# A hybrid decoder layer in float32: the input projection of the second half by seven block products over two quarters, its mixers as background jobs

## The chip, the cores and the metric

One core of a Trainium2 chip runs the whole layer in one launch. The metric is device time in microseconds. PE is the matmul engine (TensorE), DVE is VectorE, ACT is ScalarE, POOL is GpSimd, and SP issues most of the transfers. Bulk data lies in device memory (DRAM) and is worked on in the on-chip buffer (SBUF); PE writes into eight banks of PSUM.

## The reference, cut to what matters

```python
h = rmsnorm(x, norm_mix)                     # x: 2048 rows x 1024
z = h @ w_in                                 # 1024 -> 512 pool, 512 conv value, 512 conv gate, 512 u, 512 v, 3 x 1024 gates
y_a = pool_mixer(z_pool, pool_w, pool_scale) # causal means over 2, 4, 8, 16 rows, then 4 groups of 128 -> 256
y_b = silu(layernorm(causal_dwconv31(val * sigmoid(gate)))) @ conv_pw
y_c = (gelu(u) * (tril(sgu_w) @ layernorm(gelu(v)) + sgu_b)) @ sgu_out   # per chunk of 128 rows, 4 heads
x = x + (g0 * y_a + g1 * y_b + g2 * y_c) @ w_out      # g = sigmoid(z_gate + b_gate)
h = rmsnorm(x, norm_ffn)
g, val = split(h @ ffn_up)                   # 1024 -> 2 x 2816
x = x + (silu(causal_dwconv3(g)) * val) @ ffn_down
out = rmsnorm(x, norm_final)
```

## The kernel before

The sequence is cut into four quarters of 512 rows; two quarters make a half. A tile is 128 channels by 512 rows. Every product of float32 numbers is made of three matmuls: both operands are split into a rounded high part and the rest (`split`, L333, for activations; `ensure`, L188, for weights, where ScalarE casts raw into whi and VectorE subtracts it into wlo), and `mm3` (L288) issues high x high, high x low, low x high. `col` (L295) adds up eight blocks of 128 for one output tile.

Order of work: mixers and w_out for quarters 0, 1 and 2; the up projection of the first half (quarters 0 and 1); the down projection of quarter 0; mixers and w_out of quarter 3; down of quarter 1; up of the second half; down of quarters 2 and 3. The program order of PE and of SP is that in which Python emits the instructions; for the other engines a scheduler at build time picks among ready instructions the one emitted first (weights have priority, L204).

`mixers` (L586) takes one quarter through w_in and the three mixers: conv value and gate columns, then the 31 taps of the causal convolution, each a VectorE instruction over a tile (`conv_taps`, L502, queued in `bg` and issued by `drain`, L240); v and u by `rows` (L312), which makes rows of 128 positions, so that the layer norm over channels is along a row; pool columns, gates, and the products with sgu_out, conv_pw and w_out. Quarter 0 splits its weights and stores half of the split ones in a cache in DRAM, quarter 1 the other half; quarters 2 and 3 read only that cache.

`strassen` (L911) multiplies a half by the up weights with the seven-product scheme of Winograd: the left operand is a 2 x 2 of blocks (two quarters by two halves of the 1024 inputs), as is the weight (two halves of inputs by two column tiles, one pair of 22). Seven products p1 to p7 of half depth, 4 blocks each, take the place of eight. The blocks of the left operand (a11, a12, a22 and four sums s1 to s4, 4 x 2 tiles each) are made from the normed input in a background job (`rows_job`, L853), spilled to DRAM and fetched by `fetch_block` (L833). The weight sums are subtractions on POOL (L171). The order of products is written out by hand:

```python
out += [("p6", i), ("p4", i - 1), ("p5", i), ("p1", n), ("p7", i), ("p2", n), ("p3", i - 1)]
```

One PSUM bank collects p1, p6, p7 and p4 of a pair; after p1, p6 and p7 ScalarE copies what stands there (L944, L951, L954), and only then may the next product be added. VectorE adds the copies to the other products (L947, L955, L961). `ffn_gate` (L968) does the three-tap convolution on VectorE (L976 to L980) and Silu on ScalarE (L981).

Background jobs are Python generators that stand in one queue; `tick` (L252) takes one step of the first, if enough of the 69 SBUF tiles of the arena are free (`room`, L244; while the stage is "in", 56 are kept for the seven blocks). A step emits its instructions for all engines there and then. `spill` (L267) and `flush` (L271) issue a store on SP two steps after its data was emitted; SP runs in order, so a load behind a store waits with it. `need` (L1106) runs jobs until a flag is set.

## Time and profile before

| | us |
|---|---|
| median of 3 runs | 2791.51 (2787.82 to 2795.47) |
| the profiled execution | 2792.74 |
| its span, first to last instruction | 2791.0 |
| PE busy | 2753.0 |
| DVE busy | 1819.1 |
| ACT busy | 966.2 |
| POOL busy | 446.4 |

The 2792.74 us are the whole execution, the span what the trace covers. Busy time of PE counts pipelined matmuls with modelled ends, so a PE that is always busy need not be at its best pace; the pace is read from starts of matmuls. A row of a group gives busy time, the mean length of one, and the idle time of the engine before it with what ended it. PEclk is the granted clock, 1.00 being 2.4 GHz. The mean granted clock was 0.994.

### The profile page before, as it was taken

To read this page: it belongs to the slowest core of one execution; us is meant where nothing else is said; L and a number is where in the kernel's file an instruction comes from. 1 tells how busy PE (TensorE), PEld (TensorE's weight loads), DVE (VectorE), ACT (ScalarE), POOL (GpSimd) and SP (SyncE) were. 2 spreads that over 40 slices of the span, in tenths; PEclk is the share of its full clock that TensorE was granted. 3 is DMA by queue.
4 is the path that set the end of the run, shared out by engine and by line. 5 is a ranking of instruction groups with operands and counts; after the bars stand their busy time and mean duration, and the time that the engine had idled before them with its cause. 6 is when DMAs were issued, how large, how long until landed. Compare 5 with 4: busy or idle time off the path is not lost.

```text
span 2791.0 us, 32498 instructions
## 1 busy us (share of the span) xinstructions
PE 2753.0 (99%) x11958; PEld 2231.2 (80%) x11958; DVE 1819.1 (65%) x2701; ACT 966.2 (35%) x1390; POOL 446.4 (16%) x363
## 2 busy tenths in 40 slices
PE   8999999999999999999999999999998999999998
PEld 7888888888778887888888887888886888887886
DVE  8995779447797326666676479333766766776543
ACT  4434423233132214444444312121433444435431
POOL 1000210002121003232230230000213323222020
PEclk9999999999999999999999999999999999999999
DMA  7556576677798686333336464566897333337542
GB/s 247 176 186 241 193 263 234 234 264 265 263 317 287 226 299 232 124 120 122 124 110 230 136 226 166 181 226 221 305 349 260 120 125 123 120 117 279 194 138 76
DMA packets 203456, 566.71 MB, mean 203 GB/s; under 512 B 22784, under 2 KB 24832, under 8 KB 203296
## 3 DMA queue, kind: packets, MB, share of 16 engines
q1 hardware_dynamic: 200016, 556.62, 58.1%
q0 software_dynamic: 2128, 6.96, 0.6%
q8 instruction: 94, 1.54, 0.2%
q10 hardware_dynamic: 1152, 1.05, 0.1%
q14 instruction: 66, 0.54, 0.1%
HBM read 427.70 MB, written 136.84 MB: 202 GB/s over the span
## 4 chain that ended last, share of the span: by engine, by line
PE 93%; DVE 4%; DMA 1%; issue 1%; ACT 0%; POOL 0%; SPq 0%; DVEq 0%; ACTq 0%; POOLq 0%
PE ps L293 31%; PE ps L291 31%; PE ps L292 31%; DVE h L514 2%; DVE h L338 0%; DMA h<-x 0%; PE ps L386 0%; DMA h<-act 0%; DVE wlo L209 0%; DVE h L572 0%; DVE h L548 0%; DMA params<-par 0%; PE ps L394 0%; PE ps L375 0%; DVE h L539 0%
## 5 line engine op out<-in xcount | busy, mean ns | idle before, releaser
L291 PE MATMUL ps<-h,whi 128*128 128x512 f32 x3648 | 1438.4, 394 | 20.1 <-ACT whi L208 8.4
L293 PE MATMUL ps<-h,wlo 128*128 128x512 f32 x3648 | 1436.7, 394 | 1.7 <-DVE wlo L209 1.7
L292 PE MATMUL ps<-h,whi 128*128 128x512 f32 x3648 | 1436.9, 394 | 0.0
L291 PEld LDWEIGHTS ps<-h,whi 128*128 128x128 f32 x3648 | 687.5, 188 | 181.6 <-ACT whi L208 9.7
L293 PEld LDWEIGHTS ps<-h,wlo 128*128 128x128 f32 x3648 | 687.6, 188 | 161.9 <-DVE wlo L209 3.3
L292 PEld LDWEIGHTS ps<-h,whi 128*128 128x128 f32 x3648 | 687.8, 189 | 159.4 <-DVE h L1128 0.5
L209 DVE TENSOR_TENSOR wlo<-raw,whi 128x1024 fp32r<-128x1024 f32 (+1 forms) x268 | 351.2, 1311 | 291.9 <-ACT whi L208 237.8
L208 ACT CAST whi<-raw 128x1024 fp32r<-128x1024 f32 (+1 forms) x268 | 262.1, 979 | 543.2 <-PE ps L292 387.8
L514 DVE SCALAR_TENSOR_TENSOR h<-cbuf,params,h 128x512 f32<-128x512 f32 x480 | 357.8, 783 | 2.4
L369 POOL TENSOR_TENSOR h<-h,h 128x512 f32<-128x512 f32 x38 | 55.9, 1470 | 1154.1 <-ACT h L368 1153.5
L337 ACT CAST h<-h 128x512 fp32r<-128x512 f32 x219 | 133.7, 620 | 294.7 <-DVE h L858 80.8
L171 POOL TENSOR_TENSOR tw<-raw 128x512 f32<-128x512 f32 x88 | 115.4, 1331 | 591.1 <-DMA raw<-wts 466.5
L338 DVE TENSOR_TENSOR h<-h,h 128x512 fp32r<-128x512 f32 x219 | 163.0, 760 | 70.5 <-ACT h L337 68.8
L701 ACT ACTIVATE h<-ps,params 128x512 f32<-128x512 f32 x96 | 65.7, 687 | 255.6 <-PE ps L293 255.5
L719 DVE TENSOR_TENSOR h<-ps,h 128x512 f32<-128x512 f32 x64 | 44.2, 690 | 163.2 <-PE ps L293 156.1
L171 POOL TENSOR_TENSOR tw<-raw,tw 128x512 f32<-128x512 f32 x88 | 129.4, 1470 | 3.4
L208 ACT CAST whi<-tw 128x1024 fp32r<-128x1024 f32 x88 | 92.3, 1051 | 99.6 <-PE ps L292 94.2
L955 DVE TENSOR_TENSOR h<-h,ps 128x512 f32<-128x512 f32 x44 | 30.3, 688 | 130.3 <-ACT h L954 130.3
L209 DVE TENSOR_TENSOR wlo<-tw,whi 128x1024 fp32r<-128x1024 f32 x88 | 107.4, 1223 | 5.6 <-PE ps L292 3.0
L291 PE MATMUL ps<-whi,h 128*128 128x512 f32 x256 | 100.9, 394 | 0.0
L293 PE MATMUL ps<-whi,h 128*128 128x512 f32 x256 | 100.8, 394 | 0.0
L292 PE MATMUL ps<-wlo,h 128*128 128x512 f32 x256 | 100.6, 393 | 0.0
(144 smaller groups left out, 1686.4 us busy)
## 6 DMA issues: line engine op xcount, KB each, us to landing
raw<-wts SPq DMA_DIRECT2D x312, 512.0 KB, 4.2
whi<-wc SPq DMA_DIRECT2D x152, 512.0 KB, 3.8
wlo<-wc SPq DMA_DIRECT2D x152, 512.0 KB, 5.0
wc<-whi SPq DMA_DIRECT2D x61, 512.0 KB, 6.3
wc<-wlo SPq DMA_DIRECT2D x61, 512.0 KB, 7.1
act<-h SPq DMA_DIRECT2D x88, 256.0 KB, 2.1
h<-act SPq DMA_DIRECT2D x88, 256.0 KB, 4.7
h<-x SPq DMA_DIRECT2D x72, 256.0 KB, 5.3
```

What stands on the lines that cost most here:

```text
L171: sub = lambda o, a, b: self.nc.gpsimd.tensor_tensor(o, a, b, op=ALU.subtract)
L208: nc.scalar.copy(h, src)
L209: nc.vector.tensor_tensor(l, src, h.bitcast(F32), op=ALU.subtract)
L291: mm(out, l[0], r[0], start=start, stop=False)
L292: mm(out, l[0], r[1], start=False, stop=False)
L293: mm(out, l[1], r[0], start=False, stop=stop)
L337: self.nc.scalar.copy(hi, src)
L338: self.nc.vector.tensor_tensor(lo, src, hi.bitcast(F32), op=ALU.subtract)
L369: eng.tensor_tensor(s, s, t, op=ALU.add)
L514: nc.vector.scalar_tensor_tensor(acc, buf[:, k:k + T], w, acc, op0=ALU.mult, op1=ALU.add)
L701: nc.scalar.activation(s, ps, AF.Sigmoid, bias=self.par("bgate", n * 8 + j))
L719: nc.vector.tensor_tensor(s[1], ps, s[1], op=ALU.mult)
```

## The change

Quarters 0 and 1 stay. For quarters 2 and 3, w_in becomes one stage (`w_in`) that runs `strassen` over both quarters with 22 pairs of w_in column tiles. What comes out is passed through its activation and stored in DRAM: the gates, u, v, the pool columns and the gated conv input. The mixers become jobs: `mix_job` (spatial mix, now on transposed v, 128 positions at a time), `pool_job`, `conv_job`, and `half_taps` for the convolution, whose taps stay in `bg` and are issued by `drain` in the stages w_in, up of the first half and down of quarter 0. `half_mixers` then does the products with sgu_out, conv_pw and w_out for both quarters in one stage, streaming its inputs from DRAM, with raw weights instead of cached ones. The normed blocks of x for w_in ("w1") are made by `factors_job` and `rows_job` during quarters 0 and 1. The blocks of the first half ("f0") are now made in jobs during w_in, which were made during quarter 2. The order of work becomes: quarters 0 and 1, w_in of the second half, up of the first half, down of quarter 0, half_mixers, down of quarter 1, up of the second half, down of quarters 2 and 3.

Besides, the seven products come in another order with less lead (LAG 1), the weight sums are made in place of the raw weights (parts ty and tx for t2 and t3), the arena has 74 larger tiles (the four conv buffers are among them at first), the high parts of blocks and most outputs of w_in are stored by DMAs that ScalarE issues (`now`), and half of the f1 blocks stay in SBUF (`direct` = 2).

```diff
-LAG = 3
+LAG = 1
...
-NHALF = 69
+NHALF = 74
...
-NJOB = 2
+NJOB = 3
+LATE = 1
 NPAIR = NFF
-BLOCKS = ("a11", "a12", "s2", "s1", "s3", "a22", "s4")
+BLOCKS = ("a11", "a12", "s2", "s3", "s1", "a22", "s4")
...
+def in_pairs():
+
+    conv = [("conv", i, 512 + i * P, 1024 + i * P) for i in range(4)]
+    uv = [("uv", i, 1536 + i * P, 2048 + i * P) for i in range(4)]
+    pool = [("pool", i, 2 * i * P, (2 * i + 1) * P) for i in range(2)]
+    tiles = list(range(8)) + list(range(16, 24)) + list(range(8, 16))
+    gate = [("gate", (m, n), 2560 + m * P, 2560 + n * P) for m, n in zip(tiles[::2], tiles[1::2])]
+    rest = uv + pool + gate
+    return [p for i in range(4) for p in (conv[i], rest[2 * i], rest[2 * i + 1])] + rest[8:]
+
...
+OF = {"p1": ("x1", 0), "p2": ("x1", 1), "p7": ("ty", 0), "p6": ("ty", 1),
+      "p5": ("tx", 0), "p4": ("tx", 1), "p3": ("b22", 0)}
+
+
+def up_order():
+
+    out = [(p, i) for i in range(LAG) for p in ("p1", "p2")]
+    for i in range(NPAIR + 1):
+        n = i + LAG
+        out += [("p4", i - 1), ("p6", i), ("p1", n), ("p2", n), ("p7", i), ("p5", i), ("p3", i - 1)]
+    return [(p, i) for p, i in out if 0 <= i < NPAIR]
...
+        self.seq = mix("put") + mix("get") + parts(1) + parts(3) + down + some(2) + down + parts(3) + down * 2
...
     def drain(self, n):
         for _ in range(min(n, len(self.bg))):
+            if self.bg[0].first and (self.room() < self.spare + 2 or not all(self.there[f] for f in self.bg[0].flags)):
+                return
             self.bg.popleft()()
...
+    def spill(self, dst, keys, t, flag=None, now=False):
+
+
+        if now:
+            self.nc.scalar.dma_start(out=dst, in_=t)
+            release(keys)
+        self.late[-1].append((None if now else dst, [] if now else keys, t, flag))
...
     def block(self, st, name, k, t):
 
         ks, p = self.split(t)
-        for d, key, s in zip(self.blocks[st][name][k], ks, p):
-            self.spill(d, [key], s.bitcast(F32), (st, name, k))
+        if k >= self.direct:
+            self.kept[name, k] = ks, p
+            self.there[st, name, k] = True
+            return
+        for n, (d, key, s) in enumerate(zip(self.blocks[st][name][k], ks, p)):
+            self.spill(d, [key], s.bitcast(F32), (st, name, k) if n else None, n == 0)
 
...
+        self.skeys[name], self.S[name] = [], []
+        for k in range(4):
+            if (name, k) in self.kept:
+                keys, p = self.kept.pop((name, k))
+            else:
+                keys, p = self.fetch(self.blocks[st][name][k], FR)
+            self.skeys[name] += keys
+            self.S[name].append(p)
...
             elif p == "p7":
-                k, t = self.half()
-                cp(t, ps)
-                tt(t, t, g["c"], op=ALU.add)
+                g["u3"] = self.half()
+                cp(g["u3"][1], ps)
+            elif p == "p5":
+                k, t = g.pop("u3")
+                tt(t, t, ps, op=ALU.add)
                 sink(i, "22", t, k)
...
+                w = self.par("cw", i * KC + k)
+                if k == 0:
+                    kb, buf = self.halves.take()
+                    nc.sync.dma_start(out=buf[:, HALO:], in_=self.ci[q][i])
+                    nc.sync.dma_start(out=buf[:, 0:HALO], in_=self.ci[q - 1][i][:, T - HALO:])
+                    ka, acc = self.half()
+                    got.append((kb, buf, ka, acc))
+                    nc.vector.tensor_scalar(acc, buf[:, 0:T], w, self.par("cb", i), op0=ALU.mult, op1=ALU.add)
+                    return
+                kb, buf, ka, acc = got[0]
+                nc.vector.scalar_tensor_tensor(acc, buf[:, k:k + T], w, acc, op0=ALU.mult, op1=ALU.add)
+                if k == KC - 1:
+                    release([kb])
+                    self.spill(self.cv[q][i], [ka], acc, ("cv", q, i))
...
+        for k in range(KC):
+            go = tap(k)
+            go.first = k == 0
+            go.flags = [("ci", n, i) for n in (q - 1, q)]
+            self.bg.append(go)
...
+        def act(dst, t, key, func, flag, **kw):
+            k, s = (key, t) if key else self.half()
+            nc.scalar.activation(s, t, func, **kw)
+            self.spill(dst, [k], s, flag, True)
...
+        def conv(i, c, t, key):
...
+                self.half_taps(i, q0)
+                if i == 3:
+                    for n in range(4):
+                        self.half_taps(n, q0 + 1)
...
+        def sink(i, c, t, key):
+            kind, m = pairs[i][:2]
+            q, y = q0 + (c[0] == "2"), c[1] == "2"
+            if kind == "conv":
+                conv(m, c, t, key)
+            elif kind == "uv":
+                act((self.us, self.vs)[y][q][:, m * T:(m + 1) * T], t, key, AF.Gelu_apprx_tanh, ("uv"[y], q, m))
+            elif kind == "gate":
+                act(self.gates[q][m[y]], t, key, AF.Sigmoid, ("gate", q, m[y]),
+                    bias=self.par("bgate", m[y]))
...
+    def mix_job(self, q, rs):
+
+
+        nc = self.nc
+        while not (self.sg and all(self.there[n, q, h] for n in "uv" for h in range(4))):
...
+            return key, t
+
+        nxt = [load(src, rs[0]) for src in (self.vs, self.us)]
+        for _ in range(4):
+            yield 1
+        for n, r in enumerate(rs):
+            (kv, vt), (ku, ut) = nxt
+            key, t = self.half()
+            ps = self.bank()
+            for h in range(4):
...
+            nc.vector.scalar_tensor_tensor(off, mv[:, 0:1], -1.0, rstd, op0=ALU.mult, op1=ALU.mult)
+            nc.scalar.activation(t, t, AF.Identity, bias=off, scale=rstd)
+            yield
+            yield 2
+            ks, x = self.split(t)
+            yield 2
+            if n + 1 < len(rs):
+                nxt = [load(src, rs[n + 1]) for src in (self.vs, self.us)]
+            yield
+            yield
+            yield
+            pm = self.bank()
+            for h in range(4):
+                hs = slice(h * P, (h + 1) * P)
+                self.mm3(pm[:, hs], (x[0][:, hs], x[1][:, hs]), (sg[0][:, hs], sg[1][:, hs]), True, True)
+            for h in range(4):
+                hs = slice(h * P, (h + 1) * P)
+                nc.vector.scalar_tensor_tensor(t[:, hs], pm[:, hs], self.par("slg", h), bt[:, hs], op0=ALU.mult, op1=ALU.add)
+            nc.vector.tensor_tensor(t, t, ut, op=ALU.mult)
+            self.spill(heads(self.gt[q])[:, :, r * P:(r + 1) * P], [key], heads(t), ("gt", q, r))
+            release(ks + [ku])
+            yield 1
...
+    def half_mixers(self, q0, during, later):
...
+            src = (gT, cT)[n]
+            for j in range(8):
+                if j % 2 == 0:
+                    w = self.take()
+                if n == 0 and j == 4:
+                    for q in qs:
+                        for i in range(4):
+                            self.need("cs", q, i)
+                    cstream = self.stream([self.cs[q][i] for q in qs for i in range(4)], 3)
+                if n == 0:
+                    acc.append([])
+                for m in range(2):
+                    ps = self.col(w, [p for _, p in src[m]], off=(j % 2) * 512, nk=4)
+                    k, s = self.gstream()
+                    if n == 0:
+                        acc[j].append(self.astream())
+                    v.tensor_tensor(s, ps, s, op=ALU.mult)
+                    ka, a = acc[j][m]
+                    (v if n and j > 5 else g).tensor_tensor(a, a, s, op=ALU.add)
+                    release([k])
+                    if n:
+                        merged[m].append(self.split(a))
+                        release([ka])
...
+        self.add(self.setup_sgd(), self.factors_job(2), self.factors_job(3))
+        self.add(self.rows_job("w1", 2, xT, "nmix", self.rstx[2:], [("rstx", 2), ("rstx", 3)]))
...
-        for q in range(3):
-            rows = next_rows(q + 1) if q < 2 else iter(range(4))
-            self.pace = 1 + (q == 2)
+        for q in range(2):
+            rows = next_rows(1) if q == 0 else iter(range(4))
+            self.pace = 1 + q
 
...
+                    self.need("w1")
+                    self.fetch_block("w1", BLOCKS[got - 1])
...
         self.stage, self.pace = "in", 1
+        self.add(self.rows_job("f0", 0, self.x1, "nffn", self.rst[:2], [("rst", 0), ("rst", 1)]))
+        self.add(self.open_mix(), *(self.mix_job(q, range(NR)) for q in (2, 3)), self.close_mix())
+        self.add(*(self.pool_job(q, range(4)) for q in (2, 3)))
 
         def near(n):
             m = n + TOTAL
-            self.fetch_rest("f0", m, (0, 0))
+            self.fetch_rest("w1", m, (0, 0))
             self.tick()
+            self.drain(1)
+            self.next_blocks("f0", n)
+
+        self.w_in(2, near)
+        self.add(self.conv_job(2), self.conv_job(3))
+
+        def near(n):
+            m = n + TOTAL
+            self.fetch_rest("f0", m, (0, 1))
+            self.tick()
+            self.drain(1 + (m % 4 == 0))
...
         def each(h, k):
             self.tick()
-            if h and k in (1, 6, 12, 16):
-                got["h"] = next(rows)
+            self.drain(2)
+            if h and k in (16, 18, 20):
+                self.mixers_first(2, k // 2 - 8)
...
+        self.half_mixers(2, lambda n: self.tick(), later)
+        self.direct = 2
         self.add(self.rows_job("f1", 2, self.x1, "nffn", self.rst[2:], [("rst", 2), ("rst", 3)]))
...
-            if h and k in (10, 13, 16, 19):
+            if h and k > 9 and k % 2 == 0:
                 if k == 10:
                     self.need("f1")
-                self.fetch_block("f1", BLOCKS[(k - 10) // 3])
+                self.fetch_block("f1", BLOCKS[k // 2 - 5])
...
+    def next_blocks(self, st, n):
+
+        if n == -14:
+            self.need(st)
+        for i, at in enumerate((-12, -10, -6, -5, -3)):
+            if n == at:
+                self.fetch_block(st, BLOCKS[i])
```

## Rows read from the trace of the kernel before

**Rows 1.** The page's part 1: busy time, share and instructions of each engine.
```profile
PE 2753.0 (99%) x11958; PEld 2231.2 (80%) x11958; DVE 1819.1 (65%) x2701; ACT 966.2 (35%) x1390; POOL 446.4 (16%) x363
```
**Rows 2.** The page's part 4: the chain that ended last, by engine.
```profile
PE 93%; DVE 4%; DMA 1%; issue 1%; ACT 0%; POOL 0%; SPq 0%; DVEq 0%; ACTq 0%; POOLq 0%
```
**Rows 3.** Timeline of PE, plain matmuls: start, length, instruction.
```profile
2127.11 0.39 PE L292 MATMUL ps<-h,whi 128*128 128x512 f32 x1
...
2139.63 0.39 PE L292 MATMUL ps<-h,whi 128*128 128x512 f32 x1
```
**Rows 4.** Busy time by 50 us windows: length, engines, PE clock, DMA share, GB/s.
```profile
800.00:850.00 50.00, 47.47 (x207) 38.26 (x206) 47.52 (x91) 18.78 (x33) 10.92 (x6) 0.97 0.80 266
...
1100.00:1150.00 50.00, 50.00 (x218) 40.55 (x217) 34.68 (x49) 21.05 (x28) 12.89 (x10) 1.00 0.38 126
...
1700.00:1750.00 50.00, 48.17 (x208) 38.55 (x208) 50.00 (x106) 16.72 (x39) 0.00 (x0) 0.97 0.42 148
...
2100.00:2150.00 50.00, 42.01 (x163) 32.47 (x162) 30.40 (x39) 20.20 (x27) 17.43 (x13) 0.90 0.77 276
```
**Rows 5.** Timeline of PE, 256-column matmuls near the end.
```profile
2769.76 0.29 PE L292 MATMUL ps<-h,whi 128*128 128x256 f32 x1
...
2772.70 0.28 PE L293 MATMUL ps<-h,wlo 128*128 128x256 f32 x1
```
**Rows 6.** The chain in order of time, small matmuls: start, length.
```profile
473.05 1.75 PE ps L671 x16
...
1069.77 0.79 PE ps L386 x8
```
**Rows 7.** Busy time of longer windows, columns as in rows 4.
```profile
1084.00:1508.00 424.00, 423.48 (x1823) 343.12 (x1824) 295.84 (x412) 180.17 (x244) 110.40 (x80) 1.00 0.40 133
400.00:500.00 100.00, 100.00 (x444) 81.32 (x443) 97.74 (x185) 32.09 (x58) 0.00 (x0) 1.00 0.66 225
...
1508.00:1640.00 132.00, 132.00 (x575) 107.19 (x573) 68.31 (x83) 45.09 (x62) 22.40 (x15) 1.00 0.49 166
```
**Rows 8.** Group of the taps from 400 to 500 us: busy, mean ns, idle before.
```profile
L514 DVE SCALAR_TENSOR_TENSOR h<-cbuf,params,h 128x512 f32<-128x512 f32 x77 | 54.7, 748 | 0.3
```
**Rows 9.** Groups by form, whole run: busy us, mean ns, idle before, releaser.
```profile
L338 DVE TENSOR_TENSOR h<-h,h 128x512 fp32r<-128x512 f32 x219 | 163.0, 760 | 70.5 <-ACT h L337 68.8
...
L209 DVE TENSOR_TENSOR wlo<-raw,whi 128x512 fp32r<-128x512 f32 x44 | 62.0, 1409 | 39.9 <-ACT whi L208 39.9
...
L980 DVE COPY fhalo<-h 128x2 f32<-128x2 f32 x44 | 46.4, 1054 | 1.4
...
L658 DVE SCALAR_TENSOR_TENSOR h<-ps,params,h 128x128 f32<-128x128 f32 x64 | 16.9, 352 | 0.0
...
L980 DVE COPY fhalo<-ps 128x2 f32<-128x2 f32 x44 | 7.0, 159 | 1.4
...
L171 POOL TENSOR_TENSOR tw<-raw 128x512 f32<-128x512 f32 x88 | 115.4, 1331 | 591.1 <-DMA raw<-wts 466.5 <-DVE h L1002 96.4 <-DVE h L979 28.2
```
**Rows 10.** ScalarE: two groups of the whole run, and its DMA queue's timeline.
```profile
L981 ACT ACTIVATE h<-h 128x512 f32<-128x512 f32 x88 | 55.6, 632 | 58.3 <-DVE h L979 55.9 <-DVE fhalo L980 0.3
...
L701 ACT ACT_TABLE_LOAD x8 | 10.3, 1283 | 0.1
...
2777.78 5.29 ACTq L1093 DMA_DIRECT2D out<-h  x8
```
**Rows 11.** Timelines of SP's DMA queue and of PE about 2100 us.
```profile
2090.24 12.34 SPq L285 DMA_DIRECT2D h<-f1s  x16
...
2107.81 0.79 PE L291 MATMUL ps<-h,whi 128*128 128x512 f32 x1 [5.16 <-ACT whi L208]
...
2110.73 0.63 PE L292 MATMUL ps<-h,whi 128*128 128x512 f32 x1
2111.16 0.63 PE L293 MATMUL ps<-h,wlo 128*128 128x512 f32 x1
```
**Rows 12.** The page's part 6: a DMA issue, KB, us to landing.
```profile
h<-x SPq DMA_DIRECT2D x72, 256.0 KB, 5.3
```

More of the change, by code (lines that the diff above doesn't have):

```diff
@@ L442, in load_x, with stream, more, nxt @@
         return keys, x
+    def stream(self, srcs, depth):
+        ahead = collections.deque()
+        srcs = iter(srcs)
+        def more():
+            for d in srcs:
+                (k,), (t,) = self.fetch([d])
+                ahead.append((k, t))
+                return
+        def nxt():
+            if not ahead:
+                more()
+            got = ahead.popleft()
+            more()
+            return got
+        for _ in range(depth):
+            more()
+        return nxt
     def setup(self):
@@ L849, in rstd_job, with factors_job @@
         release([s[0]])
-        self.spill(dst, [key], t, flag)
+        self.spill(dst, [key], t, flag, True)
         yield
+    def factors_job(self, q):
+        yield 3
+        s = self.half()
+        for k in range(KD):
+            keys, (t,) = self.fetch([self.aps["xT"][q, k]])
+            self.add_square(s[1], t, self.nc.gpsimd, k == 0)
+            release(keys)
+            if k % 2:
+                yield 3
+        yield from self.rstd_job(self.rstx[q], s, ("rstx", q))
     def rows_job(self, st, q0, src, gname, rst, flags):
@@ new lines, in conv_job @@
+    def conv_job(self, q):
+        nc = self.nc
+        while not all(self.there["cv", q, i] for i in range(4)):
+            yield
+        yield 4
+        ck, c = self.fetch(self.cv[q])
+        yield
+        yield
+        yield 3
+        ks, s = self.half()
+        nc.vector.tensor_tensor(s, c[0], c[1], op=ALU.add)
+        for i in (2, 3):
+            nc.vector.tensor_tensor(s, s, c[i], op=ALU.add)
+        kp, p = self.split(s)
+        for _ in range(6):
+            yield
+        ps = self.bank()
+        self.wide_sum(ps, p)
+        release(kp)
+        for t in c:
+            nc.vector.scalar_tensor_tensor(t, ps, -1.0 / (4 * P), t, op0=ALU.mult, op1=ALU.add)
+        for i in range(4):
+            self.add_square(s, c[i], nc.vector, i == 0)
+        for _ in range(4):
+            yield
+        f = self.rstd_all(s, 4 * P, LN_EPS, True)
+        next(f)
+        release([ks])
+        for _ in range(6):
+            yield
+        rstd = next(f)[1]
+        for i in range(4):
+            nc.vector.tensor_tensor(c[i], c[i], rstd, op=ALU.mult)
+            nc.scalar.activation(c[i], c[i], AF.Silu, bias=self.par("clb", i), scale=self.par("clg", i))
+            self.spill(self.cs[q][i], [ck[i]], c[i], ("cs", q, i), True)
+        yield
@@ L1104, in later @@
         yield from job
-    def need(self, *what):
-        while not self.there[what if len(what) > 1 else what[0]]:
-            assert any(self.jobs) or self.bg or self.due or self.fresh
-            for jobs in self.jobs:
-                self.step(jobs)
-            self.drain(2)
-            self.flush()
     def build(self):
         nc = self.nc
-        self.S, self.skeys, self.stage = {}, {}, "mix"
+        self.S, self.skeys, self.kept, self.direct, self.stage = {}, {}, {}, 4, "mix"
         self.spare, self.pace = 3, 1
```

374 lines of the change are left out of this document (300 added, 74 removed).

## The prediction

> **What bounds the kernel now.** I read the page's engine lines first: the matmul engine PE is busy 2753.0 of 2791.0 us, VectorE 65%, ScalarE 35%, POOL 16% [rows 1]. The chain of waits agrees: 93% of it is PE [rows 2]. As matmul records overlap, I took the real pace from the timeline: two rows 54 matmuls apart start 12.52 us apart [rows 3], so a 512-column matmul costs 0.232 us and nothing else fits between. The view by 50 us windows then shows where PE loses time: an undisturbed window holds 217 or 218 matmuls; 207 and 208 stand in the windows at 800 and 1700 us, and 163, at a granted clock of 0.90, in the one at 2100 us [rows 4]. So time is won by issuing fewer matmuls, or by mending those windows, and lost wherever another engine makes PE wait.
>
> **1. Products removed.** Each quarter's w_in is 44 output tiles x 8 blocks of the sum x 3 matmuls = 1056, or 2112 for two quarters. The new stage makes 22 pairs x 7 products x 4 blocks x 3 = 1848. 264 go, all on the path: 264 x 0.232 = **-61.2 us**. sgu_out, conv_pw and w_out keep their counts (192 + 192 + 384 for two quarters), as does pool_w (48).
>
> **2. Small matmuls.** The spatial mix goes from 24 matmuls of 512 columns (5.6 us) to 96 of 128 columns. No split product of 128 columns is in the trace. Below: 256 columns take 0.118 us (25 in 2.94 us) [rows 5], so half of that, 0.059; above: the 512-column pace, 0.232. The 16 transposes of 128 x 128, which also load new weights each time, took 1.75 us, 0.109 each [rows 6]; that is the nearest row, so 96 x 0.109 = 10.5, net +4.9 (0 to +16.7). The 32 transposes of u become 32 of v. New are 4 transposes and 2 wide sums in setup_sgd (+0.9), and four norms that go from one wide sum (2 x 0.232) to 4 one-column products and 4 transposes (8 x about 0.1 [rows 6]): four times +0.4. Together **+7.4 us**.
>
> **3. VectorE in the first up stage.** This is where the gain can be given back. The 31 causal taps of 8 conv tiles (248) used to run under quarters 2 and 3. Now one is issued per product while w_in runs (from about the 14th product: 140 of them) and 1.25 per product in the up stage behind it: the last 108 lie in its first 86 products, 86 x 12 x 0.232 = 239 us. In that stage VectorE was busy 295.84 of 424 us [rows 7], 70%, so 239 us already hold 167 us of its own work. A tap costs 0.71 us (77 in 54.7 us; the mean length of one is 0.748) [rows 8]: 108 x 0.71 = 77. The background jobs hold some 92 us of VectorE: 8 row tiles of the mix at 5.2 (3 full-width passes of 0.76, 4 x 0.35 from PSUM, 10 tiny ones of 0.16), 8 pool groups at 3.4 (4.5 passes), 2 conv norms at 12 (15 passes and the tiny ones) [rows 9]. One step of a job is taken per product, with the f0 blocks first in the queue, so I put a third, 31 us, in this stretch. 167 + 77 + 31 = 275 against 239: 36 too much. The rest of a tap chain can run as soon as its tile is loaded, so some 11 of the last chain's taps still fall in w_in (-8), and a backlog of two products (5.6 us) is harmless. That leaves 22; as a job steps only when enough buffers are free, some of the third slides into the down stage, where VectorE was busy 68 of 132 us [rows 7]. I take **+20 us**. Bounds: 0, if half the jobs lie elsewhere and short taps fit the gaps (at 400 to 500 us VectorE was busy 97.74 of 100 and PE lost nothing [rows 7]); +56, if all 92 us fall in this stage (299 + 81 + 92 of 429 us, and 13 for the 20 pool sums on POOL, half of 1.33 us each [rows 7, 9]).
> Why PE feels it: with LAG 1 the bank that collects p1, p6, p7 and p4 is added to two products after ScalarE must have copied it; it was three. ScalarE works in order, and its Silu already waits 55.9 us for VectorE [rows 10]; behind it stand that copy, then PE.
>
> **4. ScalarE in w_in.** Sigmoid and Gelu outputs alternate in the first ten pairs, and a change of table costs 1.283 us [rows 10]; some 30 of them. Outputs leave by DMAs that ScalarE issues itself, 8 of which took 5.29 us at the end of the run [rows 10]; w_in issues some 100. With weights, copies and the f0 splits that is about 17 of a pair's 19.5 us in the first ten pairs: no bound, but bursts that delay the copies of step 3. **+6 us** (0 to +20).
>
> **5. Boundaries.** The loss at 2100 us goes: there SP issued 16 block loads in 12.34 us, the next raw weights left only behind them, and PE waited 5.16 us [rows 11]. Now the loads are spread over six steps, and half of the f1 blocks never leave the chip. The window lost 55 x 0.232 = 12.8 us; I count **-9** (-12.8 to 0: the added norm jobs run just ahead of f1 and may be forced there). The f0 blocks now load at the end of w_in, 56 loads within 14 products, behind the same SP queue as the weights: **+5** (0 to +15). The losses at 800 and 1700 us belong to stages that go, 21 matmuls, **-5**; quarter 1 gets the w1 blocks as quarter 2 had f0, and half_mixers starts on streamed tiles: **+2** (-1 to +10). What hides half_mixers' loads: each product is 2.8 us and its tiles are asked for three products ahead, against 5.3 us from issue to landing of such a tile [rows 12]; were that cover gone, 32 products would wait about 2.5 us each.
> Priced at nothing: 88 outputs of w_in go out and come back at 256 KB each, 45 MB in some 850 us or 53 GB/s on top of the 133 GB/s and 0.40 of the DMA engines of the up stage [rows 7]; without that cover weights would come late, as in the windows of step 5. The w1 blocks cost VectorE 44 passes of some 0.76 us, 33 us, in quarters 0 and 1, where it is full only around the taps; quarter 2 carried the same with f0, and lost the 11 matmuls at 800 us.
>
> **Sum.** The profiled execution took 2792.7 us, 1.2 over the median of the three. -61.2 + 7.4 + 20 + 6 - 9 + 5 - 5 + 2 = -34.8; 2792.7 - 34.8 = 2757.9, which I give as 2758.
>
> **A rule against it.** A subtraction into wlo of 512 columns took 1409 ns where its twin in the splits took 760; a copy of two columns 1054 ns from SBUF but 159 from PSUM [rows 9]; both stand where POOL computes. The Trainium skill says why (GPSIMD Engine Reference, Specifications): POOL shares its SBUF interfaces with VectorE, and instructions with two SBUF inputs contend. The taps are such instructions and came into POOL's stage; this trace agrees with the rule. POOL was busy 110.4 of 424 us there [rows 7]; if a tap takes double while POOL runs, 26% of 77 us is +20, and step 3 becomes 40. That makes 2778.
>
> **Rivals.**
> A, the forecast: 2758, by itself 2744 to 2771. Chance 0.40.
> B, VectorE's surplus is hidden and PE keeps its pace: for it speaks 400 to 500 us; against it, that there no ScalarE copy stood between VectorE and the next product. 2758 - 20 = 2738. Chance 0.25.
> C, contention as above, or jobs that all fall in the stage: 2778 to 2795. Chance 0.20.
> D, slower: the chain PE, ScalarE copy, PE breaks in every pair of the up stage. VectorE's full surplus is 56, and each wait also costs clock: after the 5.16 us at 2100 us, matmuls started 0.43 us apart [rows 11], the lower of the two levels, nine of them, 9 x 0.2 = 1.8 us, in 12 to 22 pairs 22 to 40. 2758 + 36 + 30 = 2824. It decides where PE loses more than 55 us in that stage, that is when VectorE needs over 484 us for its 429. For it: the sum of step 3 at its upper end; against: every term has to lie there. Chance 0.15.
> On D the Trainium skill (TensorE: Matmul & The Clock Gate, Loop structure matters more than you think) warns that waits between bursts of matmuls bring the half clock back; the trace shows that once, at 2100 us.
> That the change does not do what it says has no place: the counts of step 1 stand in the code.
>
> **Range and chances.** 2728 to 2798 leaves out most of D (0.13) and B's lowest part (0.06); C's upper end is in. 0.3% (8.4 us) is what a measurement tells from no change; below 2783 lie A, B and a part of C, 0.70; within it the rest of C, 0.15; above it D, 0.15.
>
> **What would show it.** Right: 11500 or so matmuls on PE; in the second half of w_in 217 per 50 us; in the first 240 us of the first up stage fewer, some 200, with VectorE above 95% and PE waiting for ScalarE's copy or VectorE; no loss of 55 at the start of the last up stage. B would show 217 throughout; C and D VectorE full through the whole stage, D with a granted clock under 1. Wrong altogether would be long waits in w_in (ScalarE, or f0 forced late), or in half_mixers.

## The result: slower, and the profile after

The changed kernel took 2830.07 us (median of 4 runs, 2829.19 to 2836.09), the kernel before 2791.99 (4 runs, 2787.82 to 2795.47): a ratio of 1.0145, 95% interval 1.0129 to 1.0162. Forecast were 2758 us, with a range that ended at 2798.

Two lines of the page after: the engines [rows 1] and the chain of waits by engine [rows 2].

```profile
PE 2730.6 (97%) x11812; PEld 2206.8 (78%) x11812; DVE 1932.7 (68%) x2844; ACT 1095.0 (39%) x1551; POOL 686.4 (24%) x517
...
PE 73%; DVE 15%; DMA 5%; issue 4%; ACT 2%; POOL 1%; SPq 1%; ACTq 0%; DVEq 0%; POOLq 0%
```

PE does fewer matmuls, but the chain that ended last now runs through VectorE, transfers and ScalarE for 22% of the span, where it was 5% before [rows 2]. POOL went from 446.4 to 686.4 us; no term of the sum named that. The 50 us windows after (columns as in [rows 4]) show where PE stopped:

```profile
450.00:500.00 50.00, 45.30 (x188) 35.18 (x187) 48.03 (x101) 19.44 (x43) 8.99 (x4) 0.93 0.67 233
800.00:850.00 50.00, 42.72 (x170) 33.68 (x168) 44.64 (x52) 25.74 (x35) 18.64 (x13) 0.93 0.66 224
850.00:900.00 50.00, 41.30 (x171) 32.62 (x169) 41.06 (x46) 22.68 (x33) 22.32 (x14) 0.94 0.71 240
900.00:950.00 50.00, 44.84 (x176) 35.91 (x177) 39.52 (x53) 18.88 (x27) 18.01 (x11) 0.89 0.64 213
1200.00:1250.00 50.00, 38.79 (x157) 31.04 (x158) 30.14 (x38) 16.36 (x24) 20.16 (x15) 0.90 1.00 370
1300.00:1350.00 50.00, 46.95 (x200) 37.39 (x199) 49.59 (x67) 17.76 (x27) 20.26 (x13) 0.99 0.44 143
2100.00:2150.00 50.00, 45.21 (x183) 35.91 (x182) 29.18 (x33) 17.65 (x24) 16.71 (x13) 0.93 0.87 314
2200.00:2250.00 50.00, 50.00 (x217) 40.54 (x216) 30.83 (x48) 21.19 (x30) 16.51 (x12) 1.00 0.38 120
```

An undisturbed window still holds 217 matmuls, as in [rows 4]. The disturbed ones stand in quarter 1 (450), in the first half of w_in (800 to 950; the stage runs from some 720 to 1230), at the f0 boundary (1200, with the DMA engines full), in the first up stage (1300, VectorE full) and at 2100, milder than before. I added up, over the timeline of PE, every start of a matmul that came later than its pace allows (that of [rows 3] for 512 columns): 132 us after against 40 before. Some 90 of the 132 are waits (26 of the 40 before); the rest are matmuls that started late without one, mostly in windows where the granted clock is below 1 (0.89 at 900). The span grew by 37.0, so 92 - 37 = 55 us were saved in issued work, where steps 1 and 2 had put 61.2 - 7.4 = 54. By place the 132 are: 13 in 400 to 500, 49 in 800 to 1200, 12 in 1200 to 1250, 32 in 1250 to 1550, 8 in 2100 to 2150, and 18 elsewhere, mostly at the start and the end as before.

Now PE's waits after (instruction <- what ended the wait: us in total, times, longest):

```profile
PE ps L318 <- ACT h L1052: 30.3, 13, 5.1
PE ps L318 <- ACT h L1042: 13.2, 2, 9.4
PE ps L318 <- ACT h L1049: 8.0, 5, 3.5
```

These three are ScalarE's copies of the bank that collects p1, p6, p7 and p4 of a pair; no wait for them stood in the trace before. Why one is late, the timelines of POOL, ScalarE and PE at 842 to 853 us show (start, length, instruction, in brackets the idle time before it and what ended it):

```profile
842.86 5.65 POOL L195 TENSOR_TENSOR raw<-raw 128x512 f32<-128x512 f32 x4 [2.64 <-DMA raw<-wts]
```
```profile
847.17 1.05 ACT L228 CAST whi<-raw 128x1024 fp32r<-128x1024 f32 x1 [5.64 <-POOL raw L195]
849.56 0.62 ACT L364 CAST h<-h 128x512 fp32r<-128x512 f32 x1 [1.34 <-DVE h L957]
850.21 0.33 ACTq L293 DMA_DIRECT2D f0a<-h  x1
850.58 1.05 ACT L228 CAST whi<-raw 128x1024 fp32r<-128x1024 f32 x1 [0.40 <-PE ps L320]
851.53 0.58 ACT L1052 COPY h<-ps 128x512 f32<-128x512 f32 x1
```
```profile
849.86 0.40 PE L320 MATMUL ps<-h,wlo 128*128 128x512 f32 x1
852.16 0.50 PE L318 MATMUL ps<-h,whi 128*128 128x512 f32 x1 [1.90 <-ACT h L1052]
852.50 0.40 PE L319 MATMUL ps<-h,whi 128*128 128x512 f32 x1
```

ScalarE came to the copy only behind other work. It stood 5.64 us before a weight cast, most of it for sums that POOL made one after the other once the raw weights had landed, then 1.34 for a VectorE result; two casts and a transfer issue ran before the copy, and PE stood 1.90 us. Last, the groups by form after: weight sums on POOL, then three VectorE groups (the taps under w_in and up, those of quarters 0 and 1, and the product in the gate, 686 ns before).

```profile
L195 POOL TENSOR_TENSOR raw<-raw 128x512 f32<-128x512 f32 x264 | 373.3, 1414 | 838.0 <-DMA raw<-wts 615.2 <-DVE fhalo L1445 40.8 <-DVE h L1086 35.8
L1086 DVE SCALAR_TENSOR_TENSOR h<-h,params,h 128x512 f32<-128x512 f32 x240 | 222.7, 928 | 2.8
L591 DVE SCALAR_TENSOR_TENSOR h<-h,params,h 128x512 f32<-128x512 f32 x240 | 182.5, 798 | 0.6
L1467 DVE TENSOR_TENSOR h<-h,h 128x512 f32<-128x512 f32 x88 | 84.5, 961 | 24.2 <-ACT h L1446 23.0
```

The sums went from 176 (two groups of 88, [rows 9] shows one) to 264. The mean tap is 798 ns in quarters 0 and 1, where POOL does little, and 928 under w_in and up. Tap by tap, over the timelines of VectorE and POOL: of these 240, the 164 that overlap no sum on POOL take 747 ns on average, the 76 that overlap one 1318.

### The profile page after: what moved, and what is told of

It is laid out like the page before. It is cut to its first block, busy times and chain, and to the rows that moved or that the text cites. A ratio compares the mean times of both kernels' runs of the same rounds, so it can differ in the third digit from the quotient of the medians.

```text
span 2828.0 us, 33196 instructions
## 1 busy us (share of the span) xinstructions
PE 2730.6 (97%) x11812; PEld 2206.8 (78%) x11812; DVE 1932.7 (68%) x2844; ACT 1095.0 (39%) x1551; POOL 686.4 (24%) x517
## 4 chain that ended last, share of the span: by engine, by line
PE 73%; DVE 15%; DMA 5%; issue 4%; ACT 2%; POOL 1%; SPq 1%; ACTq 0%; DVEq 0%; POOLq 0%
PE ps L318 24%; PE ps L320 24%; PE ps L319 24%; DVE h L1086 3%; DVE wlo L229 3%; DVE h L591 2%; DVE h L365 1%; DMA h<-ci 1%; DMA f0s<-h 1%; DMA raw<-wts 1%; ACT whi L228 1%; DMA h<-xT 0%; POOL raw L195 0%; DVE h L957 0%; DVE h L1467 0%
## 5 line engine op out<-in xcount | busy, mean ns | idle before, releaser
L318 PE MATMUL ps<-h,whi 128*128 128x512 f32 (+1 forms) x3672 | 1458.5, 397 | 59.4 <-ACT h L1052 30.3
L320 PE MATMUL ps<-h,wlo 128*128 128x512 f32 (+1 forms) x3672 | 1455.0, 396 | 1.9 <-DVE wlo L229 1.9
L319 PE MATMUL ps<-h,whi 128*128 128x512 f32 (+1 forms) x3672 | 1451.4, 395 | 0.0
L229 DVE TENSOR_TENSOR wlo<-raw,whi 128x1024 fp32r<-128x1024 f32 x460 | 559.1, 1217 | 329.7 <-ACT whi L228 320.6
L228 ACT CAST whi<-raw 128x1024 fp32r<-128x1024 f32 x460 | 452.7, 987 | 741.7 <-PE ps L319 543.1
L195 POOL TENSOR_TENSOR raw<-raw 128x512 f32<-128x512 f32 x264 | 373.3, 1414 | 838.0 <-DMA raw<-wts 615.2
L1086 DVE SCALAR_TENSOR_TENSOR h<-h,params,h 128x512 f32<-128x512 f32 x240 | 222.7, 928 | 2.8
L591 DVE SCALAR_TENSOR_TENSOR h<-h,params,h 128x512 f32<-128x512 f32 x240 | 182.5, 798 | 0.6
L1045 DVE TENSOR_TENSOR h<-h,ps 128x512 f32<-128x512 f32 x66 | 45.2, 685 | 125.4 <-PE ps L320 104.8
L1467 DVE TENSOR_TENSOR h<-h,h 128x512 f32<-128x512 f32 x88 | 84.5, 961 | 24.2 <-ACT h L1446 23.0
L395 ACT ACTIVATE h<-h 128x512 f32<-128x512 f32 (+1 forms) x99 | 58.3, 611 | 89.9 <-DVE h L1417 29.0
L1061 DVE TENSOR_TENSOR h<-h,ps 128x512 f32<-128x512 f32 x66 | 45.1, 684 | 62.8 <-PE ps L320 62.7
L1042 ACT COPY h<-ps 128x512 f32<-128x512 f32 x66 | 38.6, 584 | 95.6 <-PE ps L320 81.7
L1049 ACT COPY h<-ps 128x512 f32<-128x512 f32 x66 | 38.6, 586 | 88.0 <-PE ps L320 79.1
```

Of the source, the lines that this page charges most:

```text
L195: sub = lambda o, a, b: self.nc.gpsimd.tensor_tensor(o, a, b, op=ALU.subtract)
L228: nc.scalar.copy(h, src)
L229: nc.vector.tensor_tensor(l, src, h.bitcast(F32), op=ALU.subtract)
L318: mm(out, l[0], r[0], start=start, stop=False)
L319: mm(out, l[0], r[1], start=False, stop=False)
L320: mm(out, l[1], r[0], start=False, stop=stop)
```

## Experiments

Three theories. **T1**: the chain PE, ScalarE's copy, PE is too short with two products between. **T2**: VectorE has more work than time. **T3**: POOL is the cause, since its sums slow VectorE beside them (contention) and reach ScalarE late (lateness). Experiments 1 to 8 are single runs beside one of the kernel before (2791.94); as its runs spread by 8 us, I read no difference under that in them. From 9 on each is a median of at least 4 runs. "Loss" is PE's time over its pace, counted as above (after: 132 us, 2830).

**1. Three products between copy and use.**

```diff
-        out += [("p4", i - 1), ("p6", i), ("p1", n), ("p2", n), ...
+        out += [("p6", i), ("p4", i - 1), ("p1", n), ("p2", n), ...
```

> Swaps p4 of the pair before and p6, so that three products instead of two lie between p6 and p7 and between p7 and p4 of one bank; all else as in the changed kernel (span 2828.0 us, PE waits for ScalarE's copies L1042, L1049, L1052 51.5 us in 20 waits). Theory 1 (the chain PE, ScalarE copy, PE is too short for how late ScalarE runs): these waits fall below 20 us and the time to 2785 to 2805. Theory 2 (VectorE has more work than time in w_in and the first up stage): the order changes nothing in the amount of work, waits stay or move, 2820 to 2835. Theory 3 (POOL is the late engine): ScalarE still waits for POOL, a part is hidden, 2810 to 2825.

Measured 2830.21, loss 134. PE's waits:

```profile
PE ps L320 <- DVE wlo L229: 19.8, 16, 4.3
...
PE ps L318 <- ACT whi L228: 12.1, 6, 3.8
...
PE ps L318 <- ACT h L1052: 7.3, 3, 3.7
```

The waits for L1052 fell from 30.3 to 7.3 us, and about as many came for the weights whi and wlo, which hang on the same sums and the same ScalarE. T1 alone falls: the chain is only where the lateness first shows. The time itself lies in T2's range, above T3's.

**2. Three taps of 31 in quarters 2 and 3** (28 of 31 taps of their convolution are left out).

```diff
-        for k in range(KC):
+        for k in (0, 1, KC - 1):
```

> Leaves out 28 of the 31 taps of the convolution in quarters 2 and 3 (224 VectorE instructions, some 180 us of VectorE). Theory 2: the loss in the first up stage (about 32 us) and half of that in w_in (about 49 us) go, 2765 to 2785. Theory 1: ScalarE's waits for VectorE shorten, those for POOL stay, 2790 to 2810. Theory 3: the loss stays apart from VectorE's share, 2810 to 2830.

Measured 2773.17, loss 75. Two of its windows:

```profile
850.00:900.00 50.00, 44.70 (x179) 34.91 (x178) 32.67 (x36) 23.23 (x34) 23.56 (x15) 0.93 0.71 244
1300.00:1350.00 50.00, 50.00 (x218) 40.61 (x217) 40.88 (x60) 20.87 (x32) 18.30 (x13) 1.00 0.48 161
```

The time lies in T2's range. The up stage is whole (218), so its loss hangs on the taps, as step 3 said, and between 800 and 1250 us the loss fell from 61 to 35. But at 850 us PE still has only 179, with VectorE busy 32.67 of 50: T2 can't be the whole cause there.

**3. The f0 sums and the pooled means on VectorE.**

```diff
-        v, g = self.nc.vector, self.nc.gpsimd
+        v, g = self.nc.vector, self.nc.vector if st == "f0" else self.nc.gpsimd
...
-            nc.gpsimd.tensor_tensor(dst[:, lo:n], ...
+            nc.vector.tensor_tensor(dst[:, lo:n], ...
```

> Moves the 16 sums of the f0 blocks and the 20 sums of the pool job from POOL to VectorE, so that POOL has only the weight sums in w_in and the first up stage. Theory 3: ScalarE no longer waits for POOL behind jobs, the loss in w_in falls by 25 to 35 us, 2795 to 2805. Theory 2: VectorE gets 25 us more work where it is full, 2835 to 2850. Theory 1: waits change cause, not sum, 2815 to 2835.

Measured 2808.49: 22 us faster with more work on VectorE. Against T2, for T3, though short of T3's range: the loss fell by 10 us between 800 and 1250 us and by 11 in the up stage, where 25 to 35 were expected of w_in alone.

**4. Taps of the up stage at half the products.**

```diff
-            self.drain(1 + (m % 4 == 0))
+            self.drain(1 - m % 2)
```

> Issues the taps in the first up stage at 0.5 instead of 1.25 per product, so that some 30 of them move into the down stage. Theory 2: the loss in the first up stage falls from 32 to 10 to 15 us, 2805 to 2815. Theories 1 and 3: VectorE is one of the things ScalarE waits for, 2815 to 2828.

Measured 2815.68: 14 us faster; the loss of the up stage (here 1250 to 1575) fell from 32 to 19. Step 3 is a part of the loss and not the largest.

**5. All 264 weight sums on VectorE.**

```diff
-        sub = lambda o, a, b: self.nc.gpsimd.tensor_tensor(o, a, b, op=ALU.subtract)
+        sub = lambda o, a, b: self.nc.vector.tensor_tensor(o, a, b, op=ALU.subtract)
```

> Moves the 264 weight sums (373 us of POOL) to VectorE (264 x 0.69 = 182 us more there); POOL keeps the jobs' sums. Theory 2 (VectorE has too much work, counted by its own instructions): 88 x 0.69 = 61 us more in w_in and in each up stage, where it is full; 2860 to 2900. Theory 3 (a sum on POOL costs VectorE as much as it saves, and comes late as well): the tap's mean falls from 928 towards 780 ns, the loss falls or stays, 2795 to 2825.

Measured 2790.36, 40 us faster. Its engine line, and three groups:

```profile
PE 2715.1 (97%) x11812; PEld 2197.7 (79%) x11812; DVE 2003.0 (72%) x3108; ACT 1098.9 (39%) x1551; POOL 316.7 (11%) x253
```
```profile
L1086 DVE SCALAR_TENSOR_TENSOR h<-h,params,h 128x512 f32<-128x512 f32 x240 | 190.3, 793 | 1.3
L195 DVE TENSOR_TENSOR raw<-raw 128x512 f32<-128x512 f32 x264 | 183.4, 695 | 46.9 <-DMA raw<-wts 41.3 <-issue 1.2
L1467 DVE TENSOR_TENSOR h<-h,h 128x512 f32<-128x512 f32 x88 | 61.3, 697 | 4.3 <-ACT h L1446 2.9
```

VectorE took on 183.4 us of sums and grew by 70.3: its other work got 113 us shorter, 0.43 us per sum that left POOL. A sum itself takes 0.695 us there instead of 1.414. T2's forecast of a slower kernel fails; T3 stands, and gave more back than its own range said.

**6. Experiment 3, with all taps of w_in and up spread thinner** (`drain(int(n % 4 != 0))` in w_in, `drain(int(m % 5 < 2))` in up).

> The sums of the f0 blocks and of the pool job on VectorE (as in e3_f0_pool_on_dve, 2808.5) and the taps spread: 0.75 per product in w_in, 0.4 in the first up stage, the rest at 2 per step in the down stage. Theory 2: about 35 taps leave w_in and about 45 the up stage, 75 us of VectorE where it is full; the loss falls by 20 to 30 us more, 2778 to 2790. If contention with the weight sums alone sets the loss (theory 3), little more falls: 2798 to 2808.

Measured 2825.26, outside both ranges. The up stage lost only 6 us, but 18 came at 1800 to 1850 and 6 at 1600, where the conv jobs, late now, were forced; a wait that the trace after had at 2.7 us grew to this:

```profile
PE ps L413 <- DVE h L396: 10.0, 3, 7.6
```

The taps have a date: spread too thin, they are paid for behind.

**7. Experiments 3 and 5 together.**

> Both moves: weight sums and the jobs' sums (f0, pool) on VectorE; in w_in and the first up stage POOL has next to nothing. Theory 2: 85 us more VectorE in those stages, 2870 to 2910. Theory 3: no contention is left, a tap costs 0.78, 2790 to 2815.

Measured 2783.40, loss 85: w_in lost about 10 instead of 49. What was left: 12 in 400 to 500, 23 in 1300 to 1450, 10 at 2050, 10 at 1150 to 1250. One window of the 23:

```profile
1300.00:1350.00 50.00, 44.01 (x182) 34.66 (x181) 46.52 (x81) 18.61 (x27) 0.00 (x0) 0.97 0.49 166
```

POOL does nothing here and PE still loses, with VectorE nearly full of taps and of the sums it took over. In the up stage, then, T2 has a part beside T3; experiment 9, which thins the taps, shows how much.

**8. Experiment 6, with the w1 steps of quarter 0 and 1 at the same pace** (`self.pace = 2` for `1 + q`).

> e6_jobs_dve_taps_spread and two job steps per product already in quarter 0, so that the w1 blocks are further on when quarter 1's taps come. If the 13 us that quarter 1 loses at 440 to 500 us (PE waits for VectorE and ScalarE there) come from w1 steps among the taps, 8 to 12 us of them go: 8 to 12 below e6. If they come from the weights and taps alone, as e6 within 4 us.

Measured 2832.99, outside both ranges. The loss at 400 to 500 went and some 25 us came in quarter 0: it follows the w1 job, which sums on POOL, wherever that stands.

**9. Experiment 7 with experiment 4's half rate.**

> All the sums of weights, of the boundary f0 and of the pooled means on VectorE (as in the run before with these three edits, 2783.4), and the taps of the joined stage drawn in every second unit. Theory 3 (GpSimd late and contending) with theory 2 for the up stage alone: of the 23 us that the joined stage still loses in 1300-1450, the half rate gives back the 13 that it gave back with GpSimd's sums in place: 2768 to 2774. Rival: both edits mend the same loss, since the taps were long only beside GpSimd's sums: 2780 to 2786.

Measured 2755.76 (2755.34 to 2757.51), ratio to the kernel before 0.9873 (0.9858 to 0.9888), loss 59, 12 us below what was expected, since the half rate gave back 28 and not 13. In 1250 to 1550 nothing was lost any more.

**10. Experiment 9 with experiment 1's order.**

> The same, and the order of the block products changed so that one more product lies between the copy that frees a block and the product that reads it. Theory 1 (the pair of two products is too short for the chain TensorE, ScalarE, TensorE) now has nothing late on GpSimd to hide behind: of the 10 us that w_in still loses it gives back 5 or more: 2764 to 2769 if the run before it gives 2771, in any case 5 below it. Rival: what is left there is VectorE's, and the order makes no difference: within 3 us of the run before it.

Measured 2752.93 (2751.50 to 2758.31), loss 58: 2.8 us, inside the spread. T1 is not seen even with POOL out of the way.

**11. Experiment 9 with the sums of w1 and f1 on VectorE as well.**

```diff
-        v, g = self.nc.vector, self.nc.vector if st == "f0" else self.nc.gpsimd
+        v, g = self.nc.vector, self.nc.vector
```

> The first of these four, and the row sums of the w1 and f1 boundaries on VectorE as well. Theory 3: the 13 us lost at 400-500 in quarter 1 and the 10 at 2050-2100 are waits on late GpSimd sums in a job: 8 to 15 us below the first of these four. Rival (theory 2): those stretches have VectorE full with taps, and more sums there cost as much as they save: within 3 us of it, or up to 8 above.

Measured **2734.58** (2730.14 to 2739.75), ratio to the kernel before 0.9802 (0.9786 to 0.9818): the best version, 21 us below experiment 9 and 95 below the change as it was made. Loss 34, less than the 40 of the kernel before; about 15 of it is still in w_in, half of that at the f0 boundary with the DMA share at 1.00. The engine line, and windows that answer to those after:

```profile
PE 2694.1 (99%) x11812; PEld 2188.5 (80%) x11812; DVE 2007.5 (74%) x3176; ACT 1100.5 (40%) x1551; POOL 195.7 (7%) x185
```
```profile
450.00:500.00 50.00, 50.00 (x230) 40.94 (x230) 50.00 (x107) 23.19 (x46) 0.00 (x0) 1.00 0.63 208
800.00:850.00 50.00, 50.00 (x218) 40.59 (x217) 46.19 (x68) 26.82 (x39) 0.00 (x0) 1.00 0.84 280
...
1300.00:1350.00 50.00, 50.00 (x217) 40.51 (x216) 49.11 (x84) 22.27 (x31) 0.00 (x0) 1.00 0.54 172
...
2100.00:2150.00 50.00, 50.00 (x218) 40.57 (x217) 37.30 (x62) 21.22 (x29) 0.00 (x0) 1.00 0.41 127
```

VectorE is as full as before or fuller (50.00 of 50 at 450), POOL at zero, and PE keeps its pace in these windows. Nor are transfers the cause of the loss at 800: the DMA share there is 0.84, against 0.66 after. So a full VectorE can cost nothing; that it need not be so, experiment 7 showed at 1300, before the taps were thinned.

**12. The kernel before, its 176 weight sums on VectorE.** The edit is that of experiment 5.

> The kernel before the change, with its 176 sums of weights on VectorE instead of GpSimd. Theory 3 as it stands: in the kernel before these sums were in time and VectorE had room beside them, so the place of the sums is worth little without the change: within 6 us of 2792. Rival: sums on GpSimd cost time in this kernel wherever they stand, and the change had nothing to do with it: 10 us or more faster, 2782 or less.

Measured 2795.49 (10 runs), ratio 1.0016 (1.0007 to 1.0025). The engine line and the sums:

```profile
PE 2750.7 (99%) x11958; PEld 2229.1 (80%) x11958; DVE 1815.3 (65%) x2877; ACT 962.6 (34%) x1390; POOL 203.8 (7%) x187
```
```profile
L171 DVE TENSOR_TENSOR tw<-raw,tw 128x512 f32<-128x512 f32 x88 | 60.4, 686 | 0.1
L171 DVE TENSOR_TENSOR tw<-raw 128x512 f32<-128x512 f32 x88 | 59.8, 687 | 4.6 <-DMA raw<-wts 4.6
```

VectorE does 120.2 us of sums more and is busy 3.8 us less than in [rows 1]: on POOL each sum had cost VectorE (120.2 + 3.8) / 176 = 0.70 us of its time, as much as the sum itself. The kernel before had the contention in full, and room for it.

**13. The kernel before, with the sums of its boundaries on VectorE too.**

> The kernel before the change with its 176 weight sums and all row sums of its boundaries on VectorE. Theory 3 (GpSimd's sums cost time through what the change added beside them): the kernel before keeps its time but for the wait at 2100-2150, where row sums on GpSimd may have part: 2780 to 2795. Rival: the 57 us by which the best version beats the kernel before are the sums' place and not the change: 2750 or less.

Measured 2792.00 (10 runs), ratio 1.0000 (0.9991 to 1.0010). The 57 us by which experiment 11 beats the kernel before are the change's own (with its taps thinned), and the loss at 2100, which stays in this run, goes by the change.

**14. Experiment 11, the weight sums back on POOL.** The edit of experiment 5, undone.

> The best version so far (2734.6: all sums on VectorE, taps of the joined stage in every second unit) with the 264 weight sums back on GpSimd. If the weight sums alone carry the loss: as with the step from 2830 to 2790 before, 30 to 40 us slower, 2765 to 2775. If they were harmful only because the boundary's sums stood in GpSimd's queue ahead of them: less than 12 us slower, 2747 or less.

Measured 2778.94 (5 runs, 2769.71 to 2783.34), 44 us slower than experiment 11, loss 87. The engine line, windows (the first line of the stretch from 800 to 1250 us is of experiment 11, the second of this run), a wait of PE, and the group of ScalarE's weight casts:

```profile
PE 2715.8 (98%) x11812; PEld 2200.9 (79%) x11812; DVE 1932.1 (69%) x2912; ACT 1095.9 (39%) x1551; POOL 569.3 (20%) x449
```
```profile
800.00:1250.00 450.00, 439.51 (x1950) 357.21 (x1949) 380.21 (x647) 203.10 (x288) 0.00 (x0) 0.99 0.69 229
```
```profile
800.00:1250.00 450.00, 418.21 (x1787) 336.96 (x1786) 339.13 (x517) 185.83 (x264) 115.03 (x80) 0.95 0.65 217
...
850.00:900.00 50.00, 43.61 (x180) 34.66 (x179) 46.82 (x56) 22.83 (x32) 15.72 (x11) 0.93 0.75 258
900.00:950.00 50.00, 47.64 (x210) 38.69 (x209) 32.45 (x62) 20.09 (x30) 10.94 (x9) 0.97 0.58 179
...
1200.00:1250.00 50.00, 41.78 (x167) 32.77 (x166) 29.34 (x45) 19.80 (x27) 11.31 (x8) 0.90 0.87 300
```
```profile
PE ps L318 <- ACT h L1052: 19.1, 10, 6.0
```
```profile
L228 ACT CAST whi<-raw 128x1024 fp32r<-128x1024 f32 x394 | 412.3, 1049 | 669.3 <-PE ps L319 507.3 <-POOL raw L195 61.0 <-DMA wc<-whi 24.3
```

VectorE is busy 75 us less than in experiment 11, and less between 800 and 1250 us too (339 against 380), yet PE loses 53 us more in the profiled executions, 38 of them in that stretch. It waits for the copies again, and ScalarE, which makes them, stood 61.0 us before weight casts for POOL. So the amount of VectorE's work is not the cause; the waits point to lateness. But it is not alone: VectorE is idle over a third of the windows at 900 and 1200 (the latter the f0 boundary, with the DMA share at 0.87), and close to full at 850, where PE has only 180 matmuls. These sums come late and contend at once, and this run doesn't part the two.

**15. Experiment 11 with 264 useless sums on POOL.** Each follows a weight's split and writes a tile that nobody reads (it holds the weight's high part a little longer).

```diff
+                    for _ in range({"ty": 3, "tx": 1}.get(what, 0)):
+                        a = h[:, 0:T].bitcast(F32)
+                        nc.gpsimd.tensor_tensor(self.idle, a, a, op=ALU.subtract)
```

> The best version so far with 264 useless subtractions on GpSimd (the rounded weights minus themselves into a tile that nobody reads), beside the real ones on VectorE: GpSimd's load on VectorE without anyone waiting for its results. VectorE gets longer by some 0.5 us for each, 130 us in all, on top of the 183 us of the real sums. If contention alone makes the loss: 2760 or more, at least as much as with the real sums on GpSimd. If the lateness of the results makes it: within 12 us of 2734.6.

Measured 2788.68 (10 runs, 2784.59 to 2792.50), 54 us slower than experiment 11, loss 88. The engine line, the useless sums, the taps, and the one wait of ScalarE for these sums:

```profile
PE 2712.1 (97%) x11812; PEld 2197.8 (79%) x11812; DVE 2159.5 (78%) x3176; ACT 1096.0 (39%) x1551; POOL 599.1 (22%) x449
```
```profile
L232 POOL TENSOR_TENSOR idle<-whi 128x512 f32<-128x512 f32 x264 | 400.1, 1516 | 1064.7 <-ACT whi L228 1053.9
L1090 DVE SCALAR_TENSOR_TENSOR h<-h,params,h 128x512 f32<-128x512 f32 x240 | 205.2, 855 | 1.8
```
```profile
ACT whi L228 <- POOL idle L232: 4.4, 5, 1.5
```

Nobody reads these results, and ScalarE stood only 4.4 us in all for a tile that one of them still held. VectorE needs 2159.5 - 2007.5 = 152 us more for the same instructions, 0.58 us for each useless sum. Contention alone is enough for a loss of this size, where VectorE also holds the real sums. The loss lies where that of experiment 14 lies: 56 us from 800 to 1250 and 13 from 1250 to 1550, against 53 and 11.

## Why the prediction was wrong

The time came out 72 us above the forecast: w_in lost 43 more than its term, the up stage 12, quarter 1 11, the f0 boundary 7, and the rest adds up to about nothing.

**Steps 1 and 2 held**: 54 us forecast, 55 saved after. (The 11500 matmuls named as a sign were a slip: by these steps some 160 fewer than 11958 are left, and the page has 11812.)

**The step that failed is step 4, with what stood as priced at nothing.** Step 4 added up what ScalarE has to do in w_in, found 17 of 19.5 us per pair, and took +6, at most +20. Measured were 49. ScalarE's own work was overstated: in about the first ten pairs it was busy 99.60 of 220 us, and 116 with its transfer issues, 53% and not 87%, with 12 changes of table in the whole stage instead of 30.

```profile
735.00:955.00 220.00, 198.86 (x824) 159.23 (x823) 167.77 (x203) 99.60 (x138) 81.69 (x52) 0.95 0.68 227
```

The step counted ScalarE's work and not what ScalarE waits for in its order. Long waits in w_in, the sign that the prediction gave for being wrong altogether, are what came. And the list of covered costs left out the 88 weight sums that the seven products bring to w_in: quarters 2 and 3 had read ready weights from the cache, now each pair makes four sums on POOL, 88 x 1.414 = 124 us, in a stretch where the f0 job's sums and the pooled means (moved to POOL by the change) queue on it too. With both on VectorE (experiment 7) w_in's loss fell to 10; experiment 14 put the weight sums alone back and PE lost 53 us more, 38 of them between 800 and 1250 us.

**Step 3 named the right wait and was short in size.** PE waits for the copies of the collecting bank, with VectorE at 49.6 of 50 us, as said; +20 was forecast for the stage, 32 came, inside its bounds. The mis-sized term is the tap: 0.71 us came from a stretch in which POOL did nothing; in 1250 to 1550, beside POOL, 90 taps took 82.5 us, 82.5 - 90 x 0.71 = 19 us of VectorE more.

```profile
L1086 DVE SCALAR_TENSOR_TENSOR h<-h,params,h 128x512 f32<-128x512 f32 x90 | 82.5, 917 | 0.9
```

With POOL at rest in that stage (experiment 7) the loss was 23, close to the +20; but VectorE then made the weight sums too, so this is no clean test of the step's sum.

**The rule on the shared interfaces** (the Trainium skill, GPSIMD Engine Reference, Specifications) bears on a large part of the loss, and I gave it 0.20 and only the taps of one stage. The traces of this case agree with it: a tap that overlaps a sum on POOL takes 1318 ns against 747. The 26% longer tap worked out from POOL's share comes near 928 over 748 ns, 24%, partly by luck: 32% of the taps overlap a sum, more than the share of 26%, and such a tap takes 1.76 times as long, less than double. Experiments 5, 12 and 15 put a number on it: a sum on POOL takes 0.4 to 0.7 us of VectorE's time.

**Step 5.** Quarter 1 was to lose 2, at most 10, and lost 13, through the w1 sums on POOL (gone in experiment 11). The f0 boundary lost 12, inside its 0 to 15. The loss at 2100 went from 12.5 to 8 instead of to 3.5; with all sums on VectorE it is gone, while the same move leaves it in the kernel before, so this step's mechanism fits, hidden behind POOL.

**Rivals.** D had waits for the copies and matmuls at a lower clock after them, and with 2824 the nearest time, but partly by luck: it put them in the up stage, which lost 32 us where D asks for more than 55, and through VectorE's sum; the larger part lay in w_in and came through POOL. B's argument, that a full VectorE need not slow PE, holds in experiment 11 and fails in experiment 7, whose up stage lost 23 us with POOL empty; that its 2738 is near the 2734.6 of experiment 11 is luck, since that is another kernel.

**What stays open**: how the 95 us between the change and experiment 11 divide between lateness, contention and the taps of the up stage. Contention without lateness brought back 54 us (experiment 15), with more work on VectorE; both together 44 (experiment 14), with less; lateness without contention was not tried. The half rate of the taps was worth 28 us from experiment 7 to 9, where 23 had stood in the up stage; experiment 11 was not tried without it.

## What to carry to other kernels

Before work is moved to an engine because it is idle, price three things: its time there, what it takes from the engine that works beside it, and who waits in order behind its result; the sum that looked free on POOL took 1.41 us, cost VectorE 0.4 to 0.7 us, about the 0.69 that VectorE needs to make it itself, and held up ScalarE's copies. When a change adds a stage of a known kind, list every instruction that the kind brings, on every engine, and not only those that the diff shows: the 88 sums stood in a helper that the up stages had always used and that now ran for w_in's weights too. A wait that moves to another instruction when its slack is widened, as in experiment 1, is a symptom, and its cause is found by taking work away from one engine at a time.

## What was not expected of the hardware

A subtraction of 512 columns that POOL did in 1.3 to 1.5 us cost VectorE 0.70 us of its own time in the kernel before, so that leaving it on POOL freed nothing (VectorE 1819.1 us busy without the sums, 1815.3 with them). ScalarE's weight casts of 1024 columns did not stretch in any of these kernels: 1048 to 1051 ns on average, with POOL busy 686 us or 196.
